# A two-layer encoder on one core: all softmax probabilities of layer 1 turned by DMA, weighed two steps later, and turned queries split by token tile

## The chip, the core and the metric

The kernel runs on one core of a Trainium2 chip. The metric is the device time of one execution in microseconds (us); of the kernel before there are three timed runs and one more execution that was profiled. Five engines work side by side: TensorE (PE; its weight loads are listed as PEld), VectorE (DVE), ScalarE (ACT), GpSimd (POOL) and SyncE (SP). Each works through its own list of instructions in order; an instruction that waits holds up all that stand behind it on its engine.

## The reference

The model is an encoder of two layers over 256 tokens of width 2048. Layer 0 mixes tokens with a spatial gating MLP, layer 1 with grouped-query attention; each layer also attends with 4 heads into 256 memory tokens, and ends with a SwiGLU network. What the change touches is the attention of layer 1:

```python
def gqa_axial_attention(qkv, g_q, g_k, cos, sin):      # 12 query heads, 4 key/value heads of 128
    q, k, v = jnp.split(qkv, [TOK_WIDTH, TOK_WIDTH + KV_WIDTH], axis=-1)
    q = apply_axial_rope(rms_norm(q, g_q), cos, sin)
    k = apply_axial_rope(rms_norm(k, g_k), cos, sin)
    ...
        s = jnp.einsum('bqhgd,bkhd->bhgqk', qi, k).astype(jnp.float32) * scale
        p = jax.nn.softmax(s, axis=-1).astype(v.dtype)
        return jnp.einsum('bhgqk,bkhd->bqhgd', p, v)

def memory_attention(q_mem, mem, g_mem, w_kv, g_mq, g_mk):   # 4 heads, keys and values from the memory
    ...
    s = jnp.einsum('bshd,bmhd->bhsm', q, k).astype(jnp.float32) * (HEAD_DIM ** -0.5)
    p = jax.nn.softmax(s, axis=-1).astype(v.dtype)
    return jnp.einsum('bhsm,bmhd->bshd', p, v).reshape(B, S, MEM_WIDTH)
```

## The kernel before

All products are done in float32 by three matmuls: every operand is split into a rounded part and the rest (hi and lo), and `matmul3` (L186 to L188) adds hi·hi, lo·hi and hi·lo into one PSUM bank. The 256 tokens are two token tiles `t` of 128.

**A linear layer** (`Linear`, `linear`) streams its weights from HBM in units of 512 rows by 512 columns. ACT casts a unit to the hi half (`whi`, L270), DVE subtracts for the lo half (`wlo`, L271), each in two instructions of 128x1024; three units of hi and lo exist at a time. PE then runs 48 matmuls of 128x512 per unit into two accumulators `acc` (one for each `t`). There are four `acc` banks in all: a linear layer can't start before the readers of the accumulators of the layer but one before it are done.

**Layer 1** runs these linear layers in this order: own keys, own values, three layers of queries (`c` = 0, 1, 2; four heads each), memory queries, memory keys, memory values, and then the output projection. After each 256 rows of weights a clock ticks, and work that was put off with `later(delay, ...)` is written into the program when its tick comes; a linear layer is 8 ticks.

**An attention piece** (`attend`) handles the four heads of one query layer. Its `waits` are the ticks after the query layer at which its four steps are written. *Queries*: `queries_T` turns the queries (through `heads_T`, on PE with `transpose4`, L192, or by DMA) and splits them, four pieces of 128x256 for each token tile (L523, L524). *Scores*: for each head six matmuls, a DVE maximum (L557), a small POOL product (L558), two ACT exponentials (L562), a DVE reciprocal (L566) and two DVE products (L568) that leave the probabilities. *Turn*: the probabilities of a head are turned, by four PE transposes (L585) out of a PSUM bank, or, where `dma` is set, through `turned`: a DVE copy that separates the 16-bit halves (L199), a DMA transpose issued from ACT's queue (L200), and, three ticks later in the program, a DVE copy back (L205). Then ACT and DVE split them (L180, L181). *Weigh*: for each pair of heads 24 matmuls of 128x256 with the values, and a split of the outcome (L180, L181). The first DVE work of a memory attention is in `queries`: two products (L494), which are also the last readers of the memory queries' accumulators.

Before the change the three query layers of layer 1 turn their probabilities on PE (`waits` 5, 6, 11, 14), and the memory attention of layer 1 already turns its probabilities by DMA, with tiles of the pool `hp`.

**What sets the order.** The program text gives an order, but the Tile framework's scheduler decides, by its own running estimate, in which order the instructions of each engine stand; so an edit in one place moves others. **Tiles**: nearly everything in layer 1 lives in one pool of 36 tiles (`big`, 128x512 float32, named `a` in the listings); a new tile waits until the last reader of the tile that had its place is done. A second pool of 16 tiles, `hp` (`kept`, named `h`), holds the layer's input until the memory queries' layer has read it. In the listings `m` is a PSUM bank for scores, turned tiles and weighed values, `s` a small column.

Of the kernel before, what the change touches and what calls it, by code (L numbers as in the profile page):

```python
# [17 lines left out]
P = 128  # L18
D = 2048
S = 256  # L20
# [35 lines left out]
def encoder(ctx: ExitStack, tc: tile.TileContext, x, x_t, mem, mem_t, columns, w_in_a, g_v_a, spatial_t, w_in_b,  # L56
# [38 lines left out]
    def v4(a):  # L95
        return a.rearrange("p (c n) -> p c n", n=P)
# [87 lines left out]
    def matmul3(out, a, b, start, stop):  # L184

        nc.tensor.matmul(out, lhsT=a[0], rhs=b[0], start=start, stop=False)  # L186
        nc.tensor.matmul(out, lhsT=a[1], rhs=b[0], start=False, stop=False)  # L187
        nc.tensor.matmul(out, lhsT=a[0], rhs=b[1], start=False, stop=stop)  # L188
# [295 lines left out]
    def queries(acc, r, gain=None):  # L484

        rh = head_squares(acc, r)
        res = []
        for t in range(NT):
            nc.vector.tensor_scalar(rh[:, 4 * t:4 * t + 4], rh[:, 4 * t:4 * t + 4], r[t], None, ALU.mult)
            if gain is None:  # L490
                res.append(turning(acc[t], rope_t["c"][:, t], rope_t["s"][:, t]))
            else:
                qn = big()
                nc.vector.tensor_tensor(v4(qn), v4(acc[t]), gain.unsqueeze(1).to_broadcast([P, 4, P]), ALU.mult)  # L494
                res.append(qn)
        return res, rh
# [17 lines left out]
    def heads_T(qn, dma=False):  # L514

        hi = [big(F32R, [P, 2, S]) for _ in range(2)]
        lo = [big(F32R, [P, 2, S]) for _ in range(2)]

        def halves_of(t, whole):
            ts = slice(t * P, (t + 1) * P)  # L520
            for pr in range(2):
                src = whole[:, 2 * pr:2 * pr + 2, :]
                nc.scalar.copy(hi[pr][:, :, ts], src)  # L523
                nc.vector.tensor_tensor(lo[pr][:, :, ts], src, hi[pr][:, :, ts].bitcast(F32), ALU.subtract)  # L524

        for t in range(NT):
            if dma:
                turned(qn[t], 3, lambda whole, t=t: halves_of(t, whole), True, nc.vector.tensor_copy)
            else:
                tp = misc()  # L530
                transpose4(qn[t], tp)
                halves_of(t, v4(tp))
        return hi, lo

    def attend(qn, waits, keys, values, kv_of, kc0, parts, dma=None, home=None):


        qn, rows = qn
        by_head = rows.rearrange("p (t h) -> p h t", t=NT)
        st = {}  # L540

        def head(p, h):
            return p[0][h // 2][:, h % 2, :], p[1][h // 2][:, h % 2, :]

        def queries_T():
            st["qT"] = heads_T(qn, dma and home is None)

        def scores(pr):
            for h in (2 * pr, 2 * pr + 1):
                kp_ = head(keys(), kv_of(h))  # L550
                qp_ = head(st["qT"], h)
                sc = misc()
                for t in range(NT):
                    ts = slice(t * P, (t + 1) * P)
                    matmul3(sc[:, t * S:(t + 1) * S], (qp_[0][:, ts], qp_[1][:, ts]), kp_, True, True)
                nmx = small(2)
                nc.vector.tensor_reduce(nmx, sc.rearrange("p (t k) -> p t k", t=NT), AX.X, ALU.max, negate=True)  # L557
                nc.gpsimd.tensor_tensor(nmx, nmx, by_head[:, h], ALU.mult)  # L558
                pe = big()
                sm = small(2)  # L560
                for t in range(NT):
                    nc.scalar.activation(pe[:, t * S:(t + 1) * S], sc[:, t * S:(t + 1) * S], AF.Exp,  # L562
                                         bias=nmx[:, t:t + 1], scale=rows[:, 4 * t + h:4 * t + h + 1],
                                         accum_out=sm[:, t:t + 1])
                rcp = small(2)
                nc.vector.reciprocal(rcp, sm)  # L566
                for t in range(NT):
                    nc.vector.tensor_scalar(pe[:, t * S:(t + 1) * S], pe[:, t * S:(t + 1) * S], rcp[:, t:t + 1], None,  # L568
                                            ALU.mult)
                st["p", h] = pe  # L570

        def turn(pr):
            for h in (2 * pr, 2 * pr + 1):
                pn = st["p", h]
                if dma:
                    def halves_of(whole, h=h):
                        hi, lo = split(whole.rearrange("p (t k) n -> p k t n", t=NT), [P, 2, NT, P], home)
                        st["t", h] = [a.rearrange("p k t n -> p (k t n)") for a in (hi, lo)]

                    turned(pn, 3, halves_of, True, nc.vector.tensor_copy, home)  # L580
                    continue
                pt = misc()
                for t in range(NT):
                    for kc in range(2):
                        nc.tensor.transpose(pt[:, kc * S + t * P:kc * S + (t + 1) * P],  # L585
                                            pn[:, t * S + kc * P:t * S + (kc + 1) * P], ident)
                st["t", h] = split(pt, [P, NB])

        def weigh(pr):
            V = values()  # L590
            po = misc()
            for hh in range(2):
                h = 2 * pr + hh
                kv = kv_of(h)
                phi, plo = st["t", h]
                for kc in range(2):
                    vhi, vlo = V[kc]
                    vs, ks = slice(kv * P, (kv + 1) * P), slice(kc * S, (kc + 1) * S)
                    matmul3(po[:, hh * S:(hh + 1) * S], (vhi[:, vs], vlo[:, vs]), (phi[:, ks], plo[:, ks]),
                            kc == 0, kc == 1)  # L600
            hi, lo = split(po.rearrange("p (h s) -> p h s", h=2), [P, 2, S])
            for hh in range(2):
                for t in range(NT):
                    ts = slice(t * P, (t + 1) * P)
                    parts.put(kc0 + 2 * pr + hh, t, hi[:, hh, ts], lo[:, hh, ts])

        later(waits[0], queries_T)
        for wait, f in zip(waits[1:], (scores, turn, weigh)):
            for pr in range(2):
                later(wait + pr, lambda f=f, pr=pr: f(pr))  # L610
# [80 lines left out]
    for l in range(DEPTH):  # L691
# [121 lines left out]
                    later(1 + t, lambda u=u, t=t, c=c: turn_u(u, t, c))  # L813
        else:
            w = w_in_b[0]
            own = {}
            load_tables(1)
            m.prep(20, 2)
            acc = linear(hT, w, TOK)
# [13 lines left out]
            own["v"] = scaled(linear(hT, w, TOK + MEMW), norm.r)  # L833
            for c in range(3):
                acc = linear(hT, w, c * NB)
                attend(queries(acc, norm.r), (5, 6, 11, 14), lambda: own["k"], lambda: own["v"],
                       lambda h, c=c: (4 * c + h) // 3, 4 * c, cat)
            m.attend(linear(hT, w, TOK + 2 * MEMW), norm.r, cat, (4, 13, 16, 20), True, kept)
            m.keys()
            m.values()  # L840
# [139 lines left out]
```

## Time and profile before

| | |
|---|---|
| timed runs | 1990.16, 1991.22, 1991.87 us; median 1991.22 |
| profiled execution | 1988.33 us, of which the span of the core is 1986.5 |
| PE busy | 1975.7 us, 99% of the span |
| DVE busy | 1645.0 us, 83% |
| ACT busy | 1217.9 us, 61% |
| PE transposes L585 | 48, from 1095.7 to 1164.9 us |

The span is the time from the first to the last instruction of the core, and the views that follow count from its start. Matmuls overlap in the array, so an instruction's duration (390 ns for 128x512) is longer than the distance from one start to the next (some 227 ns); what a matmul costs is that distance. In the lists of groups a line gives code line, engine, operation, output and inputs, shapes and count; then busy time and mean duration; then the idle time of the engine just before, with what ended it. A timeline gives start, duration, engine, line and operation, with the idle time before it in brackets. L numbers are lines of the kernel before; in the changed kernel lines behind the edits stand up to 9 lower (L557 is L565 there, L566 L574, L568 L576), while L180 to L271 and L494 keep theirs.

### The profile page before, as it was taken

What the parts mean: (1) busy time and instruction counts of PE and PEld (TensorE: products, weight loads), DVE (VectorE), ACT (ScalarE), POOL (GpSimd) and SP (SyncE); (2) the same over time, 40 slices, a digit from 0 to 9 for tenths busy, and PEclk for the clock granted to TensorE, in tenths of its full rate; (3) what the DMA queues carried; (4) which work ended last, traced back from release to release, by engine and by line L of the source; (5) the groups of instructions that cost most, each with busy time, mean ns of one, the idle gap of its engine ahead of it and who ended that gap; (6) DMA issues with size and microseconds to landing.
All of it is one profiled execution on the core that took longest, in us unless ns stands there. A gap on an engine that the chain in (4) does not pass through costs nothing.

```text
span 1986.5 us, 24053 instructions
## 1 busy us (share of the span) xinstructions
PE 1975.7 (99%) x8897; PEld 1636.8 (82%) x8897; DVE 1645.0 (83%) x1755; ACT 1217.9 (61%) x1461; POOL 95.7 (5%) x148
## 2 busy tenths in 40 slices
PE   9999999999999999999999999999999999999998
PEld 7888888888888888888888888888888888888887
DVE  6658778998889989898676866699989889898987
ACT  8756455766546665466766665756665466654673
POOL 2300001000000000000020110010000000000000
PEclk9999999999999999999999999999999999999999
DMA  9867865576775777767866545657767667686674
GB/s 349 300 191 203 242 212 190 189 217 216 231 244 186 220 217 239 235 191 232 239 201 197 168 140 175 217 191 220 226 198 246 212 208 233 195 251 215 202 219 140
DMA packets 287719, 426.99 MB, mean 215 GB/s; under 512 B 93904, under 2 KB 94160, under 8 KB 287600
## 3 DMA queue, kind: packets, MB, share of 16 engines
q1 hardware_dynamic: 199808, 387.62, 58.8%
q10 hardware_dynamic: 82800, 20.91, 6.3%
q0 software_dynamic: 4992, 16.91, 3.8%
q8 instruction: 70, 1.15, 0.2%
q14 instruction: 49, 0.40, 0.1%
HBM read 394.45 MB, written 2.10 MB: 200 GB/s over the span
## 4 chain that ended last, share of the span: by engine, by line
PE 94%; DMA 2%; DVE 2%; ACT 1%; issue 1%; SPq 0%; DVEq 0%; ACTq 0%
PE acc L188 27%; PE acc L186 26%; PE acc L187 26%; PE m L188 5%; PE m L186 5%; PE m L187 5%; DMA a<-a 1%; DVE wlo L271 1%; DMA raw<-in_w_in_a 1%; PE m L192 0%; ACT whi L270 0%; PE m L722 0%; ACT junk L212 0%; PE m L585 0%; DVE T L379 0%
## 5 line engine op out<-in xcount | busy, mean ns | idle before, releaser
L271 DVE TENSOR_TENSOR wlo<-raw,whi 128x2048 fp32r<-128x2048 f32 (+2 forms) x466 | 841.4, 1821 | 202.9 <-ACT whi L270 198.8
L270 ACT CAST whi<-raw 128x2048 fp32r<-128x2048 f32 (+2 forms) x466 | 705.9, 1535 | 434.3 <-PE acc L187 294.5
L186 PE MATMUL acc<-whi,h 128*128 128x512 f32 x1440 | 561.6, 390 | 1.7 <-ACT whi L270 1.7
L187 PE MATMUL acc<-whi,h 128*128 128x512 f32 x1440 | 560.7, 389 | 0.0
L188 PE MATMUL acc<-wlo,h 128*128 128x512 f32 x1440 | 514.8, 390 | 0.1
L186 PE MATMUL acc<-whi,a 128*128 128x512 f32 x999 | 388.3, 390 | 1.0 <-DVE x L457 1.0
L187 PE MATMUL acc<-whi,a 128*128 128x512 f32 x999 | 388.6, 389 | 0.0
L188 PE MATMUL acc<-wlo,a 128*128 128x512 f32 x999 | 365.6, 390 | 0.4 <-DVE wlo L271 0.3
L188 PEld LDWEIGHTS acc<-wlo,h 128*128 128x128 f32 x1440 | 270.3, 188 | 57.9 <-DVE wlo L271 2.0
L186 PEld LDWEIGHTS acc<-whi,h 128*128 128x128 f32 x1440 | 270.4, 188 | 57.4 <-ACT whi L270 2.3
L187 PEld LDWEIGHTS acc<-whi,h 128*128 128x128 f32 x1440 | 270.4, 188 | 55.4
L188 PEld LDWEIGHTS acc<-wlo,a 128*128 128x128 f32 x999 | 187.5, 188 | 40.7 <-DVE wlo L271 2.1
L186 PEld LDWEIGHTS acc<-whi,a 128*128 128x128 f32 x999 | 187.6, 188 | 39.8 <-issue 1.4
L187 PEld LDWEIGHTS acc<-whi,a 128*128 128x128 f32 x999 | 187.6, 188 | 38.8
L270 ACT CAST whi<-T 128x1536 fp32r<-128x1536 f32 x93 | 137.8, 1481 | 119.2 <-PE acc L187 98.7
L271 DVE TENSOR_TENSOR wlo<-T,whi 128x1536 fp32r<-128x1536 f32 x93 | 162.9, 1751 | 4.7 <-PE acc L188 4.7
L379 DVE TENSOR_TENSOR T<-raw 128x1024 f32<-128x1024 f32 x93 | 113.4, 1219 | 19.8 <-DMA raw<-in_w_gate_up 19.7
L186 PE MATMUL m<-whi,a 128*128 128x512 f32 x284 | 110.7, 390 | 0.0
L187 PE MATMUL m<-whi,a 128*128 128x512 f32 x284 | 110.5, 389 | 0.0
L188 PE MATMUL m<-wlo,a 128*128 128x512 f32 x284 | 110.5, 389 | 0.0
L457 DVE TENSOR_TENSOR e<-acc,e 128x512 f32<-128x512 f32 x120 | 79.0, 684 | 1.5 <-PE acc L188 1.3
L205 ACT COPY sg<-a 128x1024 uint16<-128x1024 uint16 x44 | 51.5, 1171 | 30.7 <-DMA a<-a 30.5
(162 smaller groups left out, 1528.0 us busy)
## 6 DMA issues: line engine op xcount, KB each, us to landing
raw<-in_w_gate_up SPq DMA_DIRECT2D x352, 512.0 KB, 4.4
raw<-in_w_down SPq DMA_DIRECT2D x176, 512.0 KB, 5.1
raw<-in_w_out SPq DMA_DIRECT2D x32, 1024.0 KB, 5.3
raw<-in_w_in_a SPq DMA_DIRECT2D x24, 1024.0 KB, 8.0
raw<-in_w_in_b SPq DMA_DIRECT2D x24, 1024.0 KB, 5.1
raw<-in_w_mem_kv SPq DMA_DIRECT2D x16, 1024.0 KB, 5.2
x<-e POOLq DMA_DIRECT2D x16, 512.0 KB, 5.0
a<-in_mem_t POOLq DMA_DIRECT2D x16, 256.0 KB, 5.9
```

The costliest lines, as they stand in the source:

```text
L186: nc.tensor.matmul(out, lhsT=a[0], rhs=b[0], start=start, stop=False)
L187: nc.tensor.matmul(out, lhsT=a[1], rhs=b[0], start=False, stop=False)
L188: nc.tensor.matmul(out, lhsT=a[0], rhs=b[1], start=False, stop=stop)
L205: copy(halves, back.rearrange("p (h n) -> p n h", h=2))
L270: nc.scalar.copy(hi[:, cut], raw[:, cut])
L271: nc.vector.tensor_tensor(lo[:, cut], raw[:, cut], hi[:, cut].bitcast(F32), ALU.subtract)
L379: nc.vector.tensor_tensor(T[:, :2], raw[:, 1:4:2], w01, ALU.add)
L457: nc.vector.tensor_tensor(o[t][n], self.bank[name], o[t][n], op)
```

## The change

Three things are edited. `queries_T` no longer goes through `heads_T`: the four heads of a token tile are split at once, as 128x512 (L180, L181), and the scores take their operand from that tile; this holds for all five attention pieces of the kernel. The three query layers of layer 1 get `dma` set, so their probabilities go through `turned`; with `home` set as well, their queries still go through PE. For `c` = 0 and 1 the tiles of the turn come from the pool of 36, for `c` = 2 from `hp`. And their weighing is written at ticks 16 and 17, not 14 and 15.

```diff
         def head(p, h):
             return p[0][h // 2][:, h % 2, :], p[1][h // 2][:, h % 2, :]
 
+        def of_tokens(t, whole):
+            st["q", t] = split(whole, [P, 4, P])
+
         def queries_T():
-            st["qT"] = heads_T(qn, dma and home is None)
+            for t in range(NT):
+                if dma and home is None:
+                    turned(qn[t], 3, lambda whole, t=t: of_tokens(t, whole), True, nc.vector.tensor_copy)
+                else:
+                    tp = misc()
+                    transpose4(qn[t], tp)
+                    of_tokens(t, v4(tp))
 
         def scores(pr):
             for h in (2 * pr, 2 * pr + 1):
                 kp_ = head(keys(), kv_of(h))
-                qp_ = head(st["qT"], h)
                 sc = misc()
                 for t in range(NT):
-                    ts = slice(t * P, (t + 1) * P)
-                    matmul3(sc[:, t * S:(t + 1) * S], (qp_[0][:, ts], qp_[1][:, ts]), kp_, True, True)
+                    qp_ = [a[:, h, :] for a in st["q", t]]
+                    matmul3(sc[:, t * S:(t + 1) * S], qp_, kp_, True, True)
...
             w = w_in_b[0]
-            own = {}
+            own, late = {}, (0, 1, 2)
...
             for c in range(3):
                 acc = linear(hT, w, c * NB)
-                attend(queries(acc, norm.r), (5, 6, 11, 14), lambda: own["k"], lambda: own["v"],
-                       lambda h, c=c: (4 * c + h) // 3, 4 * c, cat)
+                attend(queries(acc, norm.r), (5, 6, 11, 16 if c in late else 14), lambda: own["k"],
+                       lambda: own["v"], lambda h, c=c: (4 * c + h) // 3, 4 * c, cat, c in late,
+                       kept if c == 2 else big)
```

How the scheduler's order moves, at the two places that matter below. A number behind a name only tells tiles apart.

**DVE, where the memory queries are taken from their accumulators (L494).** In the kernel before, they stand in the softmax of `c` = 2, right behind the products of its third head, and wait for nothing:

```order
L566 RECIPROCAL s_1522_9131<-s_1521_9128 128x2
L557 TENSOR_REDUCE s_1524_9142<-m_9135 128x2
L568 TENSOR_SCALAR a_9127<-a_9127,s_1522_9131 128x256 x2
L494 TENSOR_TENSOR a_9179<-acc_8871,a_7656 128x512
L494 TENSOR_TENSOR a_9182<-acc_8872,a_7656 128x512
L566 RECIPROCAL s_1527_9149<-s_1526_9146 128x2
L568 TENSOR_SCALAR a_9145<-a_9145,s_1527_9149 128x256 x2
L181 TENSOR_TENSOR a_9244<-m_9238,a_9243 128x512
L271 TENSOR_TENSOR wlo_9438<-raw_9435,whi_9437 128x1024 x2
```

After the change the same softmax of `c` = 2 begins with these rows (`h_9222` and `h_9223` are the planes of its first head before and after the DMA transpose; `a_9029` and `a_9034` are lo halves of turned probabilities of `c` = 1, which had been turned before):

```order
L565 TENSOR_REDUCE s_1500_8998<-m_8991 128x2
L574 RECIPROCAL s_1503_9005<-s_1502_9002 128x2
L565 TENSOR_REDUCE s_1505_9016<-m_9009 128x2
L576 TENSOR_SCALAR a_9001<-a_9001,s_1503_9005 128x256 x2
L199 COPY h_9222<-a_9001 128x1024
L271 TENSOR_TENSOR wlo_9504<-raw_9501,whi_9503 128x1024 x2
L574 RECIPROCAL s_1508_9023<-s_1507_9020 128x2
L565 TENSOR_REDUCE s_1517_9064<-m_9057 128x2
L205 COPY a_9001<-h_9223 128x1024
L576 TENSOR_SCALAR a_9019<-a_9019,s_1508_9023 128x256 x2
L181 TENSOR_TENSOR a_9029<-a_8684,a_9028 128x512
L181 TENSOR_TENSOR a_9034<-a_8702,a_9033 128x512
```

Behind these come 7 rows (two copies into planes, a reciprocal, a maximum, a pair of products and two small L504 rows), and then:

```order
L205 COPY a_9019<-h_9227 128x1024
L205 COPY a_9067<-h_9243 128x1024
L574 RECIPROCAL s_1525_9089<-s_1524_9086 128x2
L181 TENSOR_TENSOR a_9095<-a_8750,a_9094 128x512
L576 TENSOR_SCALAR a_9085<-a_9085,s_1525_9089 128x256 x2
L181 TENSOR_TENSOR a_9100<-a_8768,a_9099 128x512
L199 COPY h_9246<-a_9085 128x1024
L181 TENSOR_TENSOR a_9129<-m_9115,a_9128 128x512
L494 TENSOR_TENSOR a_9146<-acc_8842,a_7652 128x512
L494 TENSOR_TENSOR a_9149<-acc_8843,a_7652 128x512
```

The two L494 rows have moved from the third head's place to the end of the softmax of `c` = 2, behind three copies back from DMA transposes of the same piece, and the first of them now waits for PE (its tile takes the place of one that the weighing of `c` = 1 still reads).

**PE, between the memory keys' layer and the memory values' layer.** In the kernel before, the first weighing of `c` = 1 (`m_9340`) stands in the midst of the keys' layer (`acc_9184`, `acc_9185`):

```order
L186 MATMUL acc_9184<-whi_9359,a_8688 128x512
L186 MATMUL m_9340<-a_9243,a_8070 128x256
L187 MATMUL m_9340<-a_9243,a_8071 128x256
L188 MATMUL m_9340<-a_9244,a_8070 128x256
```

followed by the other nine matmuls of that weighing, and then by

```order
L187 MATMUL acc_9184<-whi_9359,a_8689 128x512
L188 MATMUL acc_9184<-wlo_9360,a_8688 128x512
L186 MATMUL acc_9184<-whi_9359,a_8688 128x512
L187 MATMUL acc_9184<-whi_9359,a_8689 128x512
L188 MATMUL acc_9184<-wlo_9360,a_8688 128x512
```

After the change the last matmuls of the keys' layer (`acc_9152`) stand ahead of the weighing of `c` = 1 (`m_9115`):

```order
L186 MATMUL acc_9152<-whi_9312,a_8656 128x512
L187 MATMUL acc_9152<-whi_9312,a_8657 128x512
L188 MATMUL acc_9152<-wlo_9313,a_8656 128x512
L186 MATMUL m_9115<-a_9028,a_8066 128x256
L187 MATMUL m_9115<-a_9028,a_8067 128x256
L188 MATMUL m_9115<-a_9029,a_8066 128x256
```

and both pairs' weighing (`m_9115`, `m_9173`) goes straight into the transposes of the memory queries (`a_9146`, from L494) and the first matmuls of the values' layer (`acc_9396`):

```order
L186 MATMUL m_9173<-a_9099,a_8070 128x256
L187 MATMUL m_9173<-a_9099,a_8071 128x256
L188 MATMUL m_9173<-a_9100,a_8070 128x256
L192 MATMUL m_9250<-ident,a_9146 128x128 x4
L186 MATMUL acc_9396<-whi_9400,a_8196 128x512
L187 MATMUL acc_9396<-whi_9400,a_8197 128x512
L188 MATMUL acc_9396<-wlo_9401,a_8196 128x512
```

So nothing of a linear layer is left between the last score of `c` = 2 and the values' layer but the 8 matmuls of `acc_9151` and `acc_9152` that stand ahead of the weighing.

## The prediction

> **What bounds the kernel now.** I read the page's busy times first, then the chain that ended last, then the stretches of layer 1's attention, then single instructions in timelines.
>
> ```profile
> span 1986.5 us, 24053 instructions
> PE 1975.7 (99%) x8897; PEld 1636.8 (82%) x8897; DVE 1645.0 (83%) x1755; ACT 1217.9 (61%) x1461; POOL 95.7 (5%) x148
> PE 94%; DMA 2%; DVE 2%; ACT 1%; issue 1%; SPq 0%; DVEq 0%; ACTq 0%
> ```
>
> PE is busy for all but 10.8 of 1986.5 us, and the chain runs over it for 94% of the span. So an instruction taken from PE is time won, and every microsecond in which PE waits is time lost; the other engines matter only where PE comes to wait for them. The stretches in which the query layers' attention runs:
>
> ```profile
> 1080.00:1100.00 20.00, 20.00 (x108) 17.11 (x107) 15.43 (x30) 17.33 (x46) 3.65 (x7) 1.00 0.41 137
> 1100.00:1120.00 20.00, 20.00 (x113) 17.33 (x112) 17.07 (x32) 13.88 (x37) 2.78 (x5) 1.00 0.67 207
> 1120.00:1140.00 20.00, 20.00 (x104) 16.84 (x104) 16.79 (x32) 11.61 (x23) 2.67 (x4) 1.00 0.36 121
> 1140.00:1160.00 20.00, 20.00 (x119) 17.64 (x118) 13.52 (x28) 14.29 (x42) 3.48 (x6) 1.00 0.41 137
> 1160.00:1180.00 20.00, 20.00 (x109) 17.07 (x108) 13.54 (x20) 13.86 (x34) 0.21 (x2) 1.00 0.43 134
> 1180.00:1200.00 20.00, 20.00 (x105) 17.11 (x104) 12.72 (x25) 8.65 (x15) 2.06 (x3) 1.00 0.58 188
> ```
>
> The columns after the length are PE, PEld, DVE, ACT and POOL busy, then clock, DMA share and GB/s. PE never waits here; DVE is busy for 89.1 of 120 us, so some 31 us are free, but these are averages.
>
> **What is removed: 48 PE transposes.** Their price is the distance between starts, not their duration:
>
> ```profile
> L585 PE MATMUL m<-ident,a 128*128 128x128 f32 x48 | 6.7, 272 | 0.0
> 1093.67 0.39 PE L188 MATMUL acc<-wlo,h 128*128 128x512 f32 x1
> ...
> 1095.71 0.39 PE L188 MATMUL acc<-wlo,h 128*128 128x512 f32 x1
> 1095.95 1.03 PE L585 MATMUL m<-ident,a 128*128 128x128 f32 x8
> 1096.74 0.48 PE L186 MATMUL acc<-whi,h 128*128 128x512 f32 x1
> 1097.05 0.40 PE L187 MATMUL acc<-whi,h 128*128 128x512 f32 x1
> ```
>
> From 1093.67 to 1095.71 there are nine matmuls of 128x512, one each 0.227 us. From 1095.71 to 1097.05 there are two such matmuls (0.45) and eight transposes, so eight cost 0.89 and one 0.11 us. 48 x 0.11 = **5.3 us less on PE**.
>
> The Trainium skill (VectorE: DVE Perf Modes, Rules for kernel authors) says to transpose a 128x128 block on TensorE where PSUM may be the destination and by DMA otherwise, and gives 390 ns against 1309 ns for a bf16 block (The three transpose paths); it speaks against this change, as a matter of latency. By its 390 ns the 48 transposes would be worth 18.7 us, an estimate; the starts in the trace say 5.3, and they decide.
>
> **What is added.** For each of 12 heads two DVE copies of 16-bit halves and one DMA transpose issued on ACT's queue. The memory attention of layer 1 does exactly this already, and its rows are the prices:
>
> ```profile
> 1196.46 0.68 DVE L557 TENSOR_REDUCE s<-m 128x2 f32<-128x512 f32 x1
> 1198.69 0.17 DVE L566 RECIPROCAL s<-s 128x2 f32<-128x2 f32 x1 [1.55 <-ACT a L562]
> 1198.78 0.67 DVE L557 TENSOR_REDUCE s<-m 128x2 f32<-128x512 f32 x1
> 1199.36 0.61 DVE L568 TENSOR_SCALAR a<-a,s 128x256 f32<-128x256 f32 x2
> 1200.01 0.69 DVE L199 COPY h<-a 128x1024 uint16<-128x1024 uint16 x1
> 1200.73 1.25 ACTq L200 DMA_TRANSPOSE h<-h  x1
> 1203.80 0.69 DVE L205 COPY a<-h 128x1024 uint16<-128x1024 uint16 x1 [0.74 <-DMA h<-h]
> 1204.41 0.16 DVE L566 RECIPROCAL s<-s 128x2 f32<-128x2 f32 x1
> 1214.46 2.35 DVE L271 TENSOR_TENSOR wlo<-raw,whi 128x1024 fp32r<-128x1024 f32 x2
> 1216.73 1.28 DVE L181 TENSOR_TENSOR h<-a,h 128x512 fp32r<-128x512 f32 x2
> DMA to landing us min/median/max: 3.0/4.7/9.9
> 1159.29 1.28 DVE L494 TENSOR_TENSOR a<-acc,a 128x512 f32<-128x512 f32 x2
> ```
>
> In distances again: a maximum 0.6; from a maximum's start to its reciprocal 2.23 (POOL and ACT lie between); a reciprocal 0.1, a pair of products 0.6, a copy 0.6 (1203.80 to 1204.41), two lo halves of weights 2.27, a split or an L494 0.6. From the issue of a transpose to the copy back it lets go: 3.07 us here, where the median of all transposes of the kernel is 4.7 and the worst 9.9. The issue itself holds ACT's queue for 1.25.
>
> The sums over layer 1: DVE gets 24 x 0.69 = 16.6 us of copies, ACT 12 x 1.25 = 15 us of issues. The split by token tile takes away: for four pieces in layer 1, 16 instructions on DVE become 8, and as many on ACT:
>
> ```profile
> L524 DVE TENSOR_TENSOR a<-m,a x24: 414/418/425, 1037.8 to 1191.3; 128x256 fp32r<-128x256 f32 x24
> L180 ACT CAST a<-m x22: 564/586/604, 185.9 to 1227.0; 128x512 fp32r<-128x512 f32 x22
> ```
>
> DVE wins 16 x 0.418 - 8 x 0.64 (1.28 for two) = 1.6 us, and ACT about as much. By these sums DVE would have 104.1 of 120 us to do, and everything could be hidden. In layer 0 the split changes only rows far ahead of the scores that read them: I count nothing.
>
> **Where it isn't hidden.** The order on DVE and PE decides. Take t = 0 as the start of the first maximum in the softmax of `c` = 2 (s_1500 in the change's rows); it waits for that head's scores. What PE has left of its own between these scores and the memory queries' transposes is, by its rows: 10 matmuls of other scores, 8 of the keys' layer, 24 of weighing.
>
> ```profile
> 1170.49 0.28 PE L186 MATMUL m<-a,a 128*128 128x256 f32 x1
> 1170.61 0.28 PE L187 MATMUL m<-a,a 128*128 128x256 f32 x1
> 1202.18 0.57 ACT L562 ACTIVATE a<-m,s,s 128x256 f32<-128x256 f32 x1 [1.18 <-POOL s L558]
> ...
> 1203.28 2.00 ACT L270 CAST whi<-raw 128x1024 fp32r<-128x1024 f32 x2
> 121.45 0.37 ACT L466 ACTIVATE junk<-acc,mem_r 128x128 f32<-128x128 f32 x1 [2.38 <-PE acc L188]
> ...
> 121.94 0.37 ACT L466 ACTIVATE junk<-acc,mem_r 128x128 f32<-128x128 f32 x1
> ```
>
> (Of ACT: two exponentials 1.1, from 1202.18 to the casts; a unit's two casts 2.0; a square 0.5.) At 0.12 for 128x256 that is 34 x 0.12 + 8 x 0.227 = **5.9 us**. Everything behind it (the transposes of L494's tile, the values' layer, whose accumulators L494 must first set free) waits for DVE to get down its list to L494, and the weighing on the way waits for splits in the same list. By hand, with the distances above:
>
> - first head: maximum 0, reciprocal 2.3, second maximum 3.0, products 3.6, copy 4.2, a pair of weight halves 6.5. ACT, after the first head's exponentials (2.3), has two squares and a unit's two casts (together 3.0) ahead of the second head's exponentials, then the cast that the weighing of `c` = 1 waits for: 5.3 + 1.1 + 0.6 = 7.0. PE ran dry at 1.2 + 1.8 = 3.0: a **first wait of 4**.
> - ACT issues the first transpose behind that cast, at 7.0; it lands at 10.1, so the copy back ends at 10.7, the second head's products at 11.2, and the lo half that PE needs for the third matmul of the weighing at 11.8. A **second wait of some 4.5**.
> - The other half 12.4, copy 13.0, reciprocal and maximum 13.8, products 14.3, copy 14.9, two small rows 15.3. The second transpose was issued at 13.1, copied back by 16.8; the third was issued at 15.0, copied back by 18.7.
> - Reciprocal, split, products, split, copy, split: 21.7; L494 22.3.
>
> So the transposes of the memory queries start at 22.4 and not at 5.9: PE waits **16.5 us**, in three or four pieces. The third and fourth transposes land under the values' layer, which then has 3.9 us of matmuls ready; I count no further wait. Before the change the same chain ran for the memory heads from 1196.46 to the last copy back, and cost nothing:
>
> ```profile
> 1218.92 0.70 DVE L205 COPY a<-h 128x1024 uint16<-128x1024 uint16 x1 [0.91 <-DMA h<-h]
> ```
>
> 22.5 us for four heads, but with the whole values' layer under it. Here that layer stands behind the chain; that cover is what is gone.
>
> Bounds. If every transpose landed at once, DVE's own list from the first maximum to L494 is 4 maxima 2.4, 4 reciprocals 0.4, 8 products 2.4, 7 copies 4.2, weight halves 2.3, 5 splits 3.0, L504 and L494 0.9: 15.6 us, a wait of 9.7. With the median landing of 4.7, two landings lie on the chain and 3.3 come on top: 19.8. The same pattern stands once more, smaller: the softmax of `c` = 1 ahead of the memory keys' layer. There DVE has 14 us of rows and PE 17.6 us of its own (linear-layer matmuls for the most part), so at best nothing is lost; with DVE held at copies back that wait for landings I allow 0 to 3 and take 1.
>
> **Sum**: -5.3 + 16.5 + 1 = +12.2 us against the profiled execution's 1988.33. That execution lies 2.9 below the median of the runs (1991.22); runs of the change should spread alike, so I add the 12.2 to the median: **2003.4**. Bounds: 1991.2 - 5.3 + 9.7 = 1995.6, and 1991.2 - 5.3 + 19.8 + 3 = 2008.7.
>
> **Rivals.**
>
> *PE's clock falls in the waits.* PE's longest wait for another engine behind its first microseconds is 1.1 us, and the granted clock is 1.00 in every stretch; but its first instructions, after an idle start, are slow:
>
> ```profile
> PE m L186 <- ACT a L523: 1.1, 1, 1.1
> 1.35 4.39 PE L748 MATMUL m<-ident 128*128 128x128 f32 x24 [1.35 <-POOL ident masks.py:199]
> ```
>
> 24 transposes of 128x128 in 4.39 us are 0.18 each against 0.11 later. If a wait of about 4 us brings that pace back, the weighing's 2.9 us and some first 3 us of the values' layer run at 0.6 of the pace: (2.9 + 3) x 0.65 = 3.8, of which the weighing's share partly lies inside waits anyway; some 3 on top, 2006.4. For it: the waits that I expect are 4 us long; against it: nothing like it occurs in this trace. The Trainium skill (TensorE: Matmul & The Clock Gate, Why this matters for your kernels) says that PE gaps over about 3 us bring the array back to half its clock; no wait in this trace is long enough to show it.
>
> *The chain is covered.* If DVE were far enough ahead of PE to reach L494 within 5.9 + 5.3 = 11.2 us of the first maximum, the change would come out even, and below that faster, down to 1991.2 - 5.3 = 1985.9. For it speak DVE's 31 free microseconds. Against it: the first maximum can't start before PE's scores, and DVE's rows alone take 15.6.
>
> *Landings as late as the worst.* Two of 9.9 instead of 3.1 would add 13.6: 2017. The DMA share of 0.43 in that stretch speaks against it.
>
> *The turn stays on PE or the order is not as listed*: then it is within 0.2% of before. The listed order shows no L585 left.
>
> **Chances.** Forecast (2003.4): 0.55. Clock (2006.4): 0.26. Late landings: 0.06. Covered: 0.08. No change: 0.05. 0.2% is 4 us, about what a measurement of this kernel can tell from no change. Slower 0.87, same 0.05, faster 0.08. The range runs from just above the lower bound, 1997, to the clock rival on top of the median landing, 2012.
>
> **What would show it.** In the profile after: no L585; PE busy below 99% of the span, with 15 us or more of PE idle where the weighing of layer 1 (L186 and L188, `m`) waits for ACT L180 and DVE L181, and L192 for DVE L494, all between the keys' and the values' layer; DVE all but full there, with idle time only ahead of L205 and L574; the same number of linear-layer matmuls at the same distance. If PE is idle there for less than 11 us the sum was wrong in its main term; if matmuls of 128x512 start 0.4 apart behind the waits, the clock rival holds.

## The result, and the profile after

The change takes 2000.46 us (median of 6 runs, 1996.97 to 2002.39) where the kernel before takes 1989.64 beside it (6 runs, 1987.4 to 1991.87): a ratio of 1.0056 with a 95% interval of 1.0046 to 1.0067, so 10.8 us slower. The forecast was 2003.4, range 1997 to 2012, and slower.

Two rows of the changed kernel's page answer to the first ones of the prediction:

```profile
span 1998.1 us, 23958 instructions
PE 1975.3 (99%) x8849; PEld 1635.6 (82%) x8849; DVE 1658.9 (83%) x1769; ACT 1216.8 (61%) x1451; POOL 95.4 (5%) x148
```

PE runs 48 instructions less and is as long busy as before; the span is 11.6 us longer. PE's waits for other engines from 1000 to 1300 us (total us, times, longest; in the kernel before there are none):

```profile
PE m L186 <- ACT a L180: 7.6, 2, 3.9
PE m L188 <- DVE a L181: 2.6, 2, 1.9
PE m L192 <- DVE a L494: 0.4, 1, 0.4
PE acc L186 <- DVE a L479: 0.4, 1, 0.4
```

Four kinds of waits are new. The first three stand between the keys' and the values' layer, where the prediction had put them. The stretches there (columns as in the prediction):

```profile
1160.00:1180.00 20.00, 9.79 (x46) 8.02 (x46) 14.96 (x32) 12.16 (x39) 2.62 (x6) 0.75 0.65 191
1180.00:1200.00 20.00, 19.57 (x104) 16.85 (x103) 14.75 (x27) 9.53 (x15) 0.00 (x0) 0.91 0.19 49
```

PE is busy for 9.79 of the 20 us from 1160, and the granted clock, 1.00 all over this part before, is 0.75 and 0.91. DVE is not full: 14.96 of 20. PE's own rows there:

```profile
1164.59 0.39 PE L188 MATMUL acc<-wlo,a 128*128 128x512 f32 x1
1168.92 0.39 PE L186 MATMUL m<-a,a 128*128 128x256 f32 x1 [3.94 <-ACT a L180]
1169.14 0.28 PE L187 MATMUL m<-a,a 128*128 128x256 f32 x1
1171.34 0.58 PE L188 MATMUL m<-a,a 128*128 128x256 f32 x1 [1.92 <-DVE a L181]
...
1173.43 0.41 PE L188 MATMUL m<-a,a 128*128 128x256 f32 x1
1177.49 0.58 PE L186 MATMUL m<-a,a 128*128 128x256 f32 x1 [3.65 <-ACT a L180]
1177.87 0.41 PE L187 MATMUL m<-a,a 128*128 128x256 f32 x1
1178.99 0.58 PE L188 MATMUL m<-a,a 128*128 128x256 f32 x1 [0.71 <-DVE a L181]
...
1181.92 1.11 PE L192 MATMUL m<-ident,a 128*128 128x128 f32 x4 [0.43 <-DVE a L494]
1182.69 0.78 PE L186 MATMUL acc<-whi,a 128*128 128x512 f32 x1
1183.26 0.58 PE L187 MATMUL acc<-whi,a 128*128 128x512 f32 x1
1183.67 0.40 PE L188 MATMUL acc<-wlo,a 128*128 128x512 f32 x1
```

The keys' layer ends at 1164.59; then come the weighing of `c` = 1 in four pieces, with a wait before each, the memory queries' transposes, and at 1182.69 the values' layer. What PE waits for is this list of DVE:

```profile
1161.98 0.69 DVE L565 TENSOR_REDUCE s<-m 128x2 f32<-128x512 f32 x1 [0.99 <-PE m L188]
1165.53 0.69 DVE L199 COPY h<-a 128x1024 uint16<-128x1024 uint16 x1
1169.47 0.69 DVE L205 COPY a<-h 128x1024 uint16<-128x1024 uint16 x1 [0.31 <-DMA h<-h]
1170.60 1.29 DVE L181 TENSOR_TENSOR a<-a,a 128x512 fp32r<-128x512 f32 x2
1175.64 0.69 DVE L205 COPY a<-h 128x1024 uint16<-128x1024 uint16 x1 [0.72 <-DMA h<-h]
1177.58 0.69 DVE L205 COPY a<-h 128x1024 uint16<-128x1024 uint16 x1 [1.25 <-DMA h<-h]
1181.19 1.28 DVE L494 TENSOR_TENSOR a<-acc,a 128x512 f32<-128x512 f32 x2
```

and, between the rows of ACT, the issues of the transposes from ACT's queue (ACTq):

```profile
1166.25 1.25 ACTq L200 DMA_TRANSPOSE h<-h  x1
1172.52 3.16 ACTq L200 DMA_TRANSPOSE h<-h  x2
```

From the first maximum of the softmax of `c` = 2 (1161.98) to L494 it is 19.2 us.

**A yardstick finer than the total.** Executions of one kernel lie several us apart (the kernel before took 1987.4 to 1997.8 us in 30 runs on one chip), because of gaps far from the change. So each profile is measured over one stretch that all kernels share: the matmuls of the linear layers (with `whi` or `wlo`) are 8457 in every trace, in the same order of layers, and the stretch runs from the start of the 4500th to that of the 5250th, counted from 0; that is 1046 to 1249 us before the change. The kernel before takes 203.40 us for it and the changed one 213.61: **+10.2 us**, nearly all of the 10.8 between the medians. Each stretch is that of one execution; the 500 matmuls of the linear layers ahead of it take 116.1 us in all twelve traces, so it is a steady measure. By the distances between starts, those 10.2 are 48 transposes less at 0.109 (-5.2), gaps of over half a us beyond the usual distance (+12.4, of which 0.5 at the start of the keys' layer), and the rest, mostly matmuls at a slower pace behind these gaps (+3.0).

### The profile page after: what moved, and what is told of

The parts are those of the page before. It is cut to its first block, busy times and chain, and to the rows that moved or that the text cites. A ratio compares the mean times of both kernels' runs of the same rounds, so it can differ in the third digit from the quotient of the medians.

```text
span 1998.1 us, 23958 instructions
## 1 busy us (share of the span) xinstructions
PE 1975.3 (99%) x8849; PEld 1635.6 (82%) x8849; DVE 1658.9 (83%) x1769; ACT 1216.8 (61%) x1451; POOL 95.4 (5%) x148
## 5 line engine op out<-in xcount | busy, mean ns | idle before, releaser
L186 PE MATMUL acc<-whi,h 128*128 128x512 f32 x1440 | 561.2, 390 | 1.6 <-ACT whi L270 1.6
L188 PE MATMUL acc<-wlo,h 128*128 128x512 f32 x1440 | 514.5, 390 | 0.5 <-DVE wlo L271 0.4
L186 PE MATMUL acc<-whi,a 128*128 128x512 f32 x999 | 388.7, 390 | 1.7 <-DVE x L457 1.3
L188 PE MATMUL acc<-wlo,a 128*128 128x512 f32 x999 | 365.2, 390 | 0.2 <-DVE wlo L271 0.2
L188 PEld LDWEIGHTS acc<-wlo,h 128*128 128x128 f32 x1440 | 270.3, 188 | 58.4 <-DVE wlo L271 2.3
L186 PEld LDWEIGHTS acc<-whi,h 128*128 128x128 f32 x1440 | 270.4, 188 | 57.3 <-ACT whi L270 2.2
L186 PEld LDWEIGHTS acc<-whi,a 128*128 128x128 f32 x999 | 187.7, 188 | 40.6 <-issue 1.7
L188 PEld LDWEIGHTS acc<-wlo,a 128*128 128x128 f32 x999 | 187.6, 188 | 40.5 <-DVE wlo L271 1.6
L186 PE MATMUL m<-whi,a 128*128 128x512 f32 x284 | 110.7, 390 | 0.0
L188 PE MATMUL m<-wlo,a 128*128 128x512 f32 x284 | 110.5, 389 | 0.0
L205 ACT COPY sg<-a 128x1024 uint16<-128x1024 uint16 x44 | 51.5, 1170 | 29.6 <-DMA a<-a 29.4
```

What stands on the lines that cost most here:

```text
L205: copy(halves, back.rearrange("p (h n) -> p n h", h=2))
```

## The experiments

Two things were open. The prediction blames the copies and issues in the softmax of `c` = 2, behind which L494 stands; but which of the three groups makes the wait? And how much of it is PE's clock?

### One group at a time

Four kernels set which query layers are turned by DMA and weighed later; the others go through PE and are weighed at 14.

```diff
-            own, late = {}, (0, 1, 2)
+            own, late = {}, ()         # e1_split_alone
+            own, late = {}, (2,)       # e2_only_c2
+            own, late = {}, (0, 1)     # e3_c0_c1
+            own, late = {}, (1,)       # e4_only_c1
```

> All three heads' groups of layer 1 back on TensorE, weighing at 14; only the split of the turned queries by token tile stays. Three theories run through this and the next three kernels. QUEUE (the prediction's): the loss is PE's wait behind the DMA-turned softmax of c = 2, whose copies stand ahead of L494. LATE: the loss comes from c = 1, whose weighing, two steps later, now falls into the softmax of c = 2 and keeps the tile that L494 needs. LOAD: each turned head costs its copies and its issue wherever it stands, 10.8 us / 12 = 0.9 us a head. For this kernel all three say the time of the kernel before, within 2 us: no transpose is saved and no wait is added. If it is slower by 4 us or more, the split itself is the cause and all three fall.

> Only c = 2 is turned by DMA (16 transposes fewer, 16 x 0.11 = 1.8 us of PE). QUEUE: the whole wait is there, some 13 us against 1.8 saved: +8 to +12 us. LATE: c = 1 weighs at 14 as before, L494 keeps its old place and PE does not wait: -1.8 us, and no wait over 0.5 us between keys' and values' layer. LOAD: 4 heads x 0.9 = +3.6 us.

> c = 0 and c = 1 turned by DMA, c = 2 back on PE (32 transposes fewer, 3.5 us). QUEUE: nothing turned stands ahead of L494: -3.5 us. LATE: the waits stay, shorter by the copies and issues of c = 2 (three copies back and three copies out, 3.6 us, and one wait for a landing): some 9 us of waits, +4 to +7 us in all. LOAD: 8 heads x 0.9 = +7.2 us, but without a PE wait over 1 us.

> Only c = 1 turned by DMA (1.8 us of transposes fewer). QUEUE: -1.8 us. LATE: its weighing stands in the softmax of c = 2 again, with PE waits for ACT L180 there: 3 to 7 us of waits, +1 to +5 us in all. LOAD: +3.6 us without such waits.

Measured against the kernel before, ratio and interval, then the stretch: the split alone 1.0007 (0.9994 to 1.002), +0.05 us; `c` = 2 alone 1.0002 (0.9992 to 1.0013), -1.8; `c` = 0 and 1 1.0035 (1.0023 to 1.0047), +8.4; `c` = 1 alone 1.0022 (1.0009 to 1.0034), +2.95. PE's waits from 1000 to 1300 us, first with `c` = 0 and 1, then with `c` = 1 alone; with the split alone and with `c` = 2 alone there is none in this list:

```profile
PE m L186 <- ACT a L180: 5.3, 2, 3.9
PE acc L186 <- DVE a L479: 1.1, 1, 1.1
PE m L188 <- DVE a L181: 0.7, 1, 0.7
```

```profile
PE m L186 <- ACT a L180: 2.6, 1, 2.6
PE m L188 <- DVE a L181: 0.8, 1, 0.8
```

So what the prediction blames does no harm alone: with `c` = 2 turned by DMA the 16 transposes are won in full, 1.8 us, or 0.11 each as the prediction had read from the starts. And with `c` = 2 back on PE 8.4 of the 10.2 us remain. The load as such (a fixed price for a head) falls too, since four heads cost -1.8 in one place and +2.95 in another. LATE fits best so far: -1.8 and +2.95 are as it said, though with `c` = 0 and 1 its 4 to 7 us became 8.4.

### Spare matmuls in the waits

```diff
             V = values()
             po = misc()
+            if kc0 == 4 and fill and dma:          # fill = (32, 28), set in layer 1
+                for _ in range(fill[pr]):
+                    nc.tensor.matmul(po[:, :P], lhsT=ident, rhs=ident, start=True, stop=True)
```

> The changed kernel with 60 spare TensorE matmuls of 128x128 (identity by identity, overwritten by what follows) ahead of the two weighings of c = 1: 32 ahead of the first, 28 ahead of the second, 6.6 us of work at 0.11 inside the waits of 4.3 and 4.1 us. The stretch named here and below runs from the start of the 4500th to the start of the 5250th of the 8457 matmuls of the linear layers, from 1046 to 1249 us; the kernel before takes it in 203.3 us and the changed one in 10.2 us more. SMALL CLOCK: the slow pace behind the waits costs only what lies after L494, four transposes at 0.77 instead of 0.44 and the first matmuls at 0.57 and 0.41 instead of 0.23: the stretch gets 0.5 to 1.0 us shorter. LARGE CLOCK (the prediction's rival): it gets some 3 us shorter. NO CLOCK: unchanged within 0.2. If the spare matmuls were in the way it gets longer.

Each spare matmul shows as two records, so 13.1 us of work were put in, twice what was meant. The time is 1.005 of before (1.0038 to 1.0062); the stretch +11.0, 0.8 more than the changed kernel, so none of the three numbers came. But 0.76 of it arises at the start of the keys' layer, where PE waits 1.1 us and not 0.4, before any spare matmul. The rows behind the waits:

```profile
1163.41 7.31 PE L602 MATMUL m<-ident 128*128 128x128 f32 x64
1170.47 0.36 PE L186 MATMUL m<-a,a 128*128 128x256 f32 x1
...
1181.02 0.66 PE L192 MATMUL m<-ident,a 128*128 128x128 f32 x4 [1.06 <-DVE a L494]
1181.43 0.47 PE L186 MATMUL acc<-whi,a 128*128 128x512 f32 x1
...
1181.97 0.40 PE L188 MATMUL acc<-wlo,a 128*128 128x512 f32 x1
```

Two things are seen. The weighing starts 7.3 us behind the keys' layer and not 4.3, and nothing is later for it by as much: L494 starts 19.7 us behind the first maximum, against 19.2. (That half a us is one issue on ACT's queue, which took 2.22 us and not 1.25.) PE is not what the chain waits for. And the pace is the usual one: from the transposes to the third matmul of the values' layer 0.95 us, where the changed kernel needed 1.75. So the slow clock costs **0.8 us** where it lies on the path; with L494 half a us later, some 0.3 are left of it from the end of the keys' layer to that third matmul (18.8 us, not 19.1). The changed kernel's weighing loses more by it: 8 distances of 0.213 behind 1171.72 and again behind 1179.37, against 0.12, and three of 0.38, 2.3 us in all; but this lies inside the waits.

### L494's tiles from another pool

```diff
-                qn = big()
+                qn = apart() if apart else big()   # layer 1's memory queries: kp, tag "sg"
```

> The changed kernel with the two tiles of L494 in layer 1 taken from the pool kp, idle there, so that L494 no longer waits for tiles that the weighing of c = 1 reads. TILE: L494 reads its accumulators early, the values' layer covers the softmax of c = 2, the waits go and the saving of 5.3 us is left: stretch -4 to -5 us against before. MOVED: DVE's list is as long as ever; with the values' layer run early, nothing covers the memory heads' turned softmax, and L627, which sets the values' accumulators free, stands behind it: a new wait of 5 to 10 us ahead of the second block of the output projection, stretch +2 to +6 us. QUEUE without the tile: as the changed kernel, +10.

> c = 0 and c = 1 turned by DMA, c = 2 on TensorE (which alone took 8.4 us more in the stretch), with L494's tiles apart as above. TILE: -3.5 us in the stretch. MOVED: the wait ahead of the weighing goes and comes back ahead of the output projection, +3 to +6 us.

With all groups turned by DMA the ratio is 1.0038 (1.0025 to 1.0051) and the stretch +5.1; with `c` = 0 and 1 1.0071 (1.0058 to 1.0085) and +11.5. PE's waits in the first:

```profile
PE acc L186 <- DVE a L627: 6.1, 1, 6.1
PE m L192 <- DVE a L508: 1.3, 1, 1.3
```

and its rows at the longest of them:

```profile
1214.32 0.39 PE L188 MATMUL acc<-wlo,a 128*128 128x512 f32 x1
1220.81 0.80 PE L186 MATMUL acc<-whi,a 128*128 128x512 f32 x1 [6.10 <-DVE a L627]
1221.40 0.63 PE L187 MATMUL acc<-whi,a 128*128 128x512 f32 x1
```

L494 now starts at 1142.1 and the values' layer right behind the keys' layer, at 1163.9. The wait ahead of the weighing is gone, and a new one of the same kind stands 50 us later: L627 and its ACT partner are the last readers of the values' accumulators, the second block of the output projection needs these, and DVE has L627 behind the memory heads' softmax. From that softmax's first maximum to the second block PE had 21.3 us of its own before the change (1196.5 to 1217.8: the end of the values' layer and 72 matmuls of the first block); here it has 8.6, against 14.1 that DVE takes to L627. So the tile was one link: freeing it moves the wait. With `c` = 2 on PE the same move made the kernel slower yet, with waits of 6.0 us for L627 and 3.5 for L508, the readers of the memory keys' accumulators; I had expected half of that.

### How far the first two groups push

```diff
-            own, late = {}, (0, 1, 2)
+            own, late = {}, (0, 2)     # e7_c0_c2
+            own, late = {}, (0,)       # e9_only_c0
+            own, late = {}, (1, 2)     # e10_c1_c2
```

> c = 0 and c = 2 turned by DMA and weighed later, c = 1 as before (32 transposes fewer). LATE: c = 1 is the piece that hurts, so L494 keeps its old place, no wait over 0.5 us between the keys' and the values' layer, stretch -3.5 us against before (and -1.8 us against c = 2 alone). LOAD: +7 us. If c = 0 has the same effect on c = 1 as c = 1 has on c = 2, a wait of some us ahead of the memory keys' layer, and the stretch comes out at or above 0.

`c` = 0 and 2: 1.0006 (0.9997 to 1.0014), stretch +3.9. This is against the theory that only `c` = 1 hurts: PE waits 3.3 us for L494, though `c` = 1 is as before. (The stretch lies above what the interval of the totals allows, -0.6 to +2.8 us, and that of `c` = 2 alone, -1.8, just below its -1.6 to +2.6; a us or two elsewhere in the program can't be ruled out.)

What the kernels differ in is read from two starts, the first maximum of the softmax of `c` = 2 on DVE and the last matmul of the keys' layer on PE. In the kernel before, 88 of the keys' layer's 96 matmuls are still to come at that maximum; they cover the softmax. In the changed one 8 are. The DVE list of the changed kernel shows what holds the scores of `c` = 2 back:

```profile
1143.03 0.69 DVE L481 TENSOR_TENSOR a<-a,a 128x512 f32<-128x512 f32 x1
1144.23 0.69 DVE L199 COPY a<-a 128x1024 uint16<-128x1024 uint16 x1
...
1149.36 0.70 DVE L205 COPY a<-a 128x1024 uint16<-128x1024 uint16 x1 [0.22 <-DMA a<-a]
...
1155.17 0.68 DVE L205 COPY a<-a 128x1024 uint16<-128x1024 uint16 x1
1158.04 0.68 DVE L181 TENSOR_TENSOR a<-m,a 128x512 fp32r<-128x512 f32 x1
```

L481 is the last step of the rotation of the queries of `c` = 2; L181 at 1158.04 is the second split of those queries, without which there are no scores. Between them stand the eight copies of `c` = 1. Before the change the same two steps were at 1133.23 and 1142.60 (L524 there): the first comes 9.8 us later, and the way from it to the second takes 5.6 us more, of which the eight copies, at 0.6 each, are 4.8. Meanwhile PE doesn't stop: it works off the keys' layer (from 1139.0, before from 1144.1). This theory, cover, was put to two more kernels:

> Only c = 0 turned by DMA and weighed later (16 transposes fewer). COVER, the theory after the eight kernels so far: PE waits for the time from the first maximum of c = 2 to L494 (the list) less the work that PE has of its own from there to the transposes of the memory queries (the cover, mostly what is left of the keys' layer). Each group weighed later pushes the scores of c = 2 back against the keys' layer: 88 of its matmuls left in the kernel before, 69 with the split alone, 33 with c = 0 and c = 2 late, 8 in the changed kernel. For this kernel the listed order has 33 left, of which 20 and 28 matmuls of 128x256 stand ahead of the first transposes: 20 x 0.227 + 28 x 0.12 = 7.9 us of cover, against a list of 11.9 (as with the split alone; c = 2 makes no copies) and 0.7 for L494 itself: a wait of 4 to 5 us, and the stretch -1.8 + 4.5 + up to 1.7 of slow clock = +2.5 to +4.5 us. ADDITIVE (c = 0 costs what it costs beside c = 2, 3.9 + 1.8 = 5.7): +5.7. LATE (only c = 1 hurts): -1.8.

> c = 1 and c = 2 turned by DMA, c = 0 as before. COVER: 45 matmuls of the keys' layer are left at the first maximum of c = 2 (42 with c = 1 alone) and L494 stands behind the whole softmax and all copies of c = 2, as in the changed kernel: 45 x 0.227 + 12 x 0.12 and the weighing's 24 x 0.12 = 14.5 us of cover against a list of 19.2 and 0.7 for L494: 5.4 us of waits, stretch -3.5 + 5.4 + up to 1.7 = +2 to +4 us. ADDITIVE (2.95 for c = 1, -1.8 for c = 2): +1.2. QUEUE (c = 2 makes the wait, whatever stands before it): +10.

`c` = 0 alone: 0.9999 (0.9983 to 1.0014), stretch -1.25, and no wait between the keys' and the values' layer. The forecast was 4 to 6 us too high: the transposes that I had read in the listed order as the memory queries' are the next rows, probabilities of `c` = 2 on PE (L593 is L585 of the kernel before), and add cover where I had ended it:

```profile
1167.41 0.60 PE L593 MATMUL m<-ident,a 128*128 128x128 f32 x4
...
1170.86 1.03 PE L593 MATMUL m<-ident,a 128*128 128x128 f32 x8
```

`c` = 1 and 2: 1.0041 (1.0028 to 1.0054), stretch +6.5 where +2 to +4 was expected; the list took 20.4 us, not 19.2, and the slow pace more than allowed. It is far from both the sum of the single ones (+1.2) and from +10. So cover, counted by hand from the listed order, missed both times: it said a loss where there was none (LATE's -1.8 came nearest there), and too small a loss in the other. What follows is read from the traces afterwards, in the order of the stretch, and was not forecast:

```
turned by DMA   keys' layer left     from the first maximum of c = 2 to      PE gaps over   stretch, of which
and weighed     at first maximum     end of keys' layer      L494            0.5 us         transposes
later           matmuls              us                      us              us             us
c = 2           69                   18.3                    14.1             0             -1.8    -1.7
c = 0           33                   11.2                    11.2             0.6           -1.25   -1.7
before          88                   26.8                    11.9             0              0       0
none (split)    69                   20.6                    11.9             0             +0.05    0
c = 1           42                    9.7                    17.5             3.8           +2.95   -1.7
c = 0, 2        33                   10.7                    13.6             4.3           +3.9    -3.5
c = 1, 2        42                    9.7                    20.4             7.4           +6.5    -3.5
c = 0, 1         8                    2.6                    14.5             8.1           +8.4    -3.5
all              8                    2.6                    19.2            12.4          +10.2    -5.2
```

(Of the gaps, 0.5 to 1.3 us stand at the start of the keys' layer wherever `c` = 0 is late.) Up to the point where L494 comes no later than the end of the keys' layer nothing is lost; from there on PE waits, for the difference less the 2.9 us of weighing where `c` = 1 is late, to within 2.2 us. Putting `c` = 2 on DMA wins 1.8 us while the cover stands, and costs 1.8 behind `c` = 0 and 1, 3.6 behind `c` = 1 and 5.2 behind `c` = 0. The split alone, which costs no time, already takes cover away: 20.6 us are left of 26.8.

## Why the prediction was right, and where it was not

**The transposes** (-5.3): right. -1.8 for 16, with no new wait of PE, is 0.11 each. By the 390 ns that the prediction quotes from the Trainium skill (VectorE: DVE Perf Modes, The three transpose paths) it would be an estimated 6.2 for 16; no run shows that as a price.

**Layer 0 and the split** (nothing): right for the time; the split alone moved the stretch by 0.05 us, and DVE's 1.6 us less were worth nothing because DVE was not waited for. But it put the scores of `c` = 2 some 4 us later against the start of the stretch, and what it took of the cover was missing when the copies came.

**The place**: right. No transposes of probabilities are left on PE; the waits are of the weighing (L186, L188) for ACT L180 and DVE L181, and of L192 for L494, between the keys' and the values' layer. DVE was not all but full, though: 14.96 of 20 us, with idle time ahead of L205, L574 and L565.

**The first of the waits** (4): 4.1 beyond the usual distance. The second (4.5): 2.1. They add up, with those that follow, to 11.9 us, where the text wanted 16.5, and by the wait rows to 10.6, which is below the 11 at which the prediction called its main term wrong. It was mis-sized in one step: the hand list had the first transpose of `c` = 2 issued at 7.0 us, behind ACT's cast for the weighing. The trace has it at 1166.25, 4.3 us behind the maximum and ahead of that cast. From issue to copy back it was 3.2 (used: 3.07), and so the copy back, the second products and L494 all came some 2.5 us earlier: the memory queries' transposes at 19.9 and not at 22.4. With PE's own 5.9 that is a wait of 14.0 us, and the records show less (11.9) because the weighing itself ran 2.3 us slower in it.

**The clock rival** (+3): the mechanism is right, its price on the path is 0.8 (spare matmuls); the 2.3 in the weighing were paid inside waits, as its text allowed for a part. The Trainium skill (TensorE: Matmul & The Clock Gate, Part 1: The HAM clock gate) says that an idle window of about 3.4 us halves the clock and that a busy one of the same length restores it, with 427 ns between starts of 512 columns when cold. In the runs a wait of 3.3 us, a little less than that window, was enough and one of 2.6 was not; the starts were 0.42 apart, as the last section shows.

**The start of the keys' layer** (1, 0 to 3): 0.5.

**The sum**: -5.2 + 14.0 + 0.8 + 0.5 = 10.1 against 10.2 measured in the stretch and 12.2 forecast. The time, 2003.4, was 2.9 too high: 1.4 because the change costs 10.8 and not 12.2, the rest because the kernel before, taken at 1991.22, took 1989.64 beside it. The lower bound of the list, a wait of 9.7, and the upper, 19.8, both held.

**The reason given** was only half of it. The prediction says that L494 moved behind three copies back of `c` = 2 and that the values' layer, which it takes for the old cover of such a chain, stands behind it. (For the memory heads that was misread: before the change the values' layer ends at 1201.3, 4.8 us into their chain, and the output projection covers the rest.) The listed order gave it the right remaining work of PE, 5.9 us. But it took that for given, and it is the larger effect: the scores of `c` = 2 come 14.5 us later (1147.44 to 1161.98) against a keys' layer that starts 5 us earlier. The cover fell from 26.8 to 2.6 us, while the list grew from 11.9 to 19.2. The table takes the fall apart: the split alone leaves 20.6 us of cover, the split with `c` = 0 late 11.2, with `c` = 1 late 9.7, with both 2.6. That these groups, far ahead of the place, decide the price is shown by `c` = 2 alone, which costs nothing, and by `c` = 0 and 1 without it, which cost 8.4. That their copies on DVE are what delays the scores is read from DVE's rows (4.8 us for `c` = 1) and not tested by itself.

**Late landings** and **covered**: neither came. The three copies back of this place started 3.1 to 3.2 us behind their issues.

What stays open: what the later weighing does by itself. It was always moved together with the turn by DMA; a turn by DMA that is weighed at 14, and a turn on PE that is weighed at 16, were not tried for `c` = 1. Nor was `c` = 2 tried with tiles from the pool of the other two. No version beat the kernel before in time; the best, `c` = 2 alone, is 1.8 us shorter in the stretch, which the totals (1.0002, 0.9992 to 1.0013) can't tell from nothing.

## What to carry to other kernels

Before a step is moved from the engine that bounds to one with free time, count the cover: how much work the bounding engine still has of its own when the lengthened chain begins, and how long the chain is up to the instruction that the next layer needs. The answer depends on what stands ahead of the place as much as on what is put there: a group that wins 1.8 us alone can cost 1.8 to 5.2 behind others, and a wait that is freed at one link can return at the next point where accumulators are handed on. Counted from the listed order alone, the cover missed twice here, by 2.5 us or more, and once in sign; it has to take in everything that stands in that order up to the first instruction that waits. Where totals scatter by several us, compare the time between two instructions that all the kernels share.

## What the runs showed of the hardware

The granted clock of PE falls behind a single long wait, and not behind a shorter one. With `c` = 0 and 2 turned by DMA there is one long wait, of 3.3 us, and the clock is 0.91 over the 20 us from 1160; with `c` = 1 alone the longest is 2.6, and it stays at 1.00:

```profile
1170.88 0.39 PE L188 MATMUL acc<-wlo,a 128*128 128x512 f32 x1
1174.61 0.63 PE L192 MATMUL m<-ident,a 128*128 128x128 f32 x4 [3.34 <-DVE a L494]
1174.99 0.58 PE L186 MATMUL acc<-whi,a 128*128 128x512 f32 x1
1175.37 0.63 PE L187 MATMUL acc<-whi,a 128*128 128x512 f32 x1
1175.79 0.63 PE L188 MATMUL acc<-wlo,a 128*128 128x512 f32 x1
...
1178.35 0.53 PE L188 MATMUL acc<-wlo,a 128*128 128x512 f32 x1
1178.72 0.39 PE L186 MATMUL acc<-whi,a 128*128 128x512 f32 x1
```

```profile
1172.49 0.39 PE L186 MATMUL m<-a,a 128*128 128x256 f32 x1 [2.64 <-ACT a L180]
1172.71 0.28 PE L187 MATMUL m<-a,a 128*128 128x256 f32 x1
```

From 1174.99 to 1178.35 eight matmuls of 128x512 start 0.42 apart, then they are back at 0.23: 1.5 us lost behind one wait of 3.3 us. Behind the wait of 6.1 us in the kernel with L494's tiles apart it is the same pace for about 3 us; behind the 2.6 us none. In all six kernels with a wait of 3.3 us or more the pace behind it is the slow one. So in these runs it is half the pace, for 3 to 4 us, from somewhere between 2.6 and 3.3 us of waiting, and a wait of just over 3 us costs PE about half as much again. Where shorter waits follow, the slow pace lasts longer: with `c` = 1 and 2, from 1173.95 to about 1182.7, with waits of 1.5 and 1.0 us in between.

I had not expected either what an issue of a transpose holds up when it waits. ACT's queue is taken from 1172.52 to 1175.68 in the changed kernel: the first issue of 1.25 us, then the second, which starts only at 1174.43, since DVE's copy out for that head runs from 1173.71 to 1174.40, then its 1.25. ACT's exponentials for the fourth head stand behind it in the same queue and start at 1175.73; the last inputs that the trace shows for them, POOL's product and DVE's L504, were there at 1174.7 and 1174.9, so the issue holds them, and the casts behind them, up by some 0.8 us. L494 is not shown to come later by it, since DVE waited meanwhile, until 1177.58, for the second of these transposes to land. So a DMA that is issued from a computing engine's queue put that engine's next work behind DVE's copy as well, here by 0.7 us.
